# Choosing each token's two experts block by block instead of for all four blocks together

## The chip, the cores and the metric

The kernel runs on one core of a Trainium2 chip. The metric is device time in microseconds (us) of one execution. A core has five engines that run side by side, each through its own list of instructions in order: TensorE (PE in the profile, with PEld for its weight loads), VectorE (DVE), ScalarE (ACT), GpSimd (POOL) and SyncE (SP), which here issues the loads of the weights. An engine that waits for a semaphore holds up all that stands behind it in its list.

## The reference

One layer of an encoder over 512 tokens (and 16 meta tokens) of width 1024: a mixer of two attention branches, then a mixture of 32 experts in 4 groups of 8. The change is in the routing of the second half:

```python
g_logits = u @ w_group + b_group                 # 4 groups
p_grp, g_sel = top_k(softmax(g_logits), 1)       # one group per token
e_logits = (u @ w_router + b_router).reshape(n, 4, 8)
e_prob = softmax(e_logits[group g_sel])          # its 8 experts
p_exp, e_sel = top_k(e_prob, 2)                  # two experts per token
gate = p_grp * p_exp / sum(p_exp)
expert = g_sel * 8 + e_sel
out = sum over the two of gate * w2[expert] @ (silu(xe @ w1[expert]) * (xe @ w3[expert]))
```

Here u is the RMS norm of the stream h after the mixer. The experts hold 201 MB of float32 weights, and all of them are read.

## The kernel before

Tokens lie on the 128 partitions, in NB = 4 blocks of 128. The kernel is written as straight code on tiles; a planner puts most instructions of each engine in order by its own costs and by priority (program order, moved ahead by `high_priority(offset=...)`), one at a time as they become ready in its plan, and that order is then fixed. Only `stage_moe` keeps PE, ACT and DVE in the order in which it is written. Tiles come from pools with a number of buffers each: a tile that finds none free waits until one is released, and with it the engine that was to write it. What matters here are H (8 buffers of 2 KB a partition), A (4, two of them held by the gather targets X), the one PSUM buffer `av` and the two PSUM buffers `tr`, and the buffers R, W and P in which the weights land.

The steps around the change, in order of time:

- `stage_o` multiplies the mixer's output by w_o (L807), adds it to h (L820), half a block of 512 columns at a time, and gives each half to `router_half`, ahead of other work by an offset of 300.
- `router_half` (8 calls: 4 blocks, 2 halves each) multiplies the half by the norm's weights on POOL (L861, into an H tile u2) and writes it to DRAM, u2d, by a DMA that POOL issues (L862); squares it on ACT (L864, junk, an A tile); turns it on PE (L867) and copies it to SBUF on DVE (L869, hT, an A tile); multiplies by the router's weights into `av` (L872). After the first half DVE saves the partial logits (L874). After the second, DVE adds both squares (L877, L878), POOL takes the power -1/2 (L880), and DVE makes the logits lg of the block, 4 of groups and 32 of experts (L881, L882).
- `choose`, at an offset of 600, once the logits of all four blocks are there: on DVE the largest group logit (L891), the index of its group (L894 to L897), the other groups' experts pushed to -1e30 (L898, L900), the 8 largest values and their indices for each block (L905, L907), the two indices as floats ef (L909), their one-hot rows eh (L912, an H tile) and the sum of the two rows, os (L914). `columns` makes two more small tables (L931 to L935). PE then counts the tokens ahead of each one by 10 small matmuls into `av` (L919, L921), and DVE makes val, each token's place in its expert (L922).
- `stage_moe` makes from val the list of the first pair's tokens (L1043, L1048, L1050), starts the gather of their rows from u2d (L1054), runs 12 matmuls that keep PE at work (`busy`, L941), makes the tables of gates and indices (`gates`, `tables`: L947 to L999, the matmuls L986), 8 more matmuls of `busy`, turns the gathered rows (L1071, copied at L1077 and L1078), and then runs 16 pairs of experts (L1086 up, L1106 down, L1117 back to the tokens).
- The weights of the experts come in pieces of 512 KB (L140 on SP) in the order in which PE takes them. Each piece needs a free buffer of its kind, so loads run ahead until all buffers are full and go on when PE has used a piece.

Of the kernel before, what the change touches and what calls it, by code (L numbers as in the profile page):

```python
# [9 lines left out]
F32 = mybir.dt.float32  # L10
F32R = mybir.dt.float32r
F16 = mybir.dt.float16
BF16 = mybir.dt.bfloat16
I32 = mybir.dt.int32
U32 = mybir.dt.uint32
AF = mybir.ActivationFunctionType
ALU = mybir.AluOpType
AX = mybir.AxisListType
# [5 lines left out]
NB = 4  # L24
# [5 lines left out]
NEG = -1e30  # L30
# [5 lines left out]
C_ID, C_I128, C_COS, C_SIN, C_TOK, C_THR, C_TOKB, C_ONCE = 0, 128, 256, 296, 336, 344, 352, 360  # L36
# [36 lines left out]
class Body:  # L73
# [753 lines left out]
    def route_setup(self):  # L827
        nc, a, cs = self.nc, self.a, self.cs
        self.g2 = self.P([128, D], F32, "gffn")
        nc.scalar.dma_start(self.g2, a["norm_ffn_g"].partition_broadcast(128))  # L830
        wr = self.H([128, 8, 36], F32, "wr0")
        nc.scalar.dma_start(wr[:, :, 0:4], a["w_group"].rearrange("(c p) n -> p c n", p=128))
        nc.scalar.dma_start(wr[:, :, 4:36], a["w_router"].rearrange("(c p) n -> p c n", p=128))
        gt = self.S([128, 8], F32, "g2t")
        with nc.allow_non_contiguous_dma(reason="small"):
            nc.scalar.dma_start(gt, a["norm_ffn_g"].rearrange("(c p) -> p c", p=128))
        self.wr = self.H([128, 8, 36], F32, "wr")
        nc.vector.tensor_tensor(self.wr, wr, gt.unsqueeze(2).to_broadcast([128, 8, 36]), ALU.mult)
        self.rt = self.cp.tile([128, 1344], F32, name="route", tag="score", bufs=1)
        self.trib = self.rt[:, 672:736].bitcast(BF16)  # L840
        nc.vector.tensor_scalar(self.trib, cs[:, C_I128:C_I128 + 128], cs[:, C_TOK:C_TOK + 1], None, op0=ALU.is_ge)
        self.onesb = self.C([128, 128], BF16, "onesb")
        nc.gpsimd.memset(self.onesb, 1.0)
        self.lg = self.rt[:, 0:144].rearrange("p (b n) -> p b n", b=NB)
        self.lgs = self.rt[:, 144:288].rearrange("p (b n) -> p b n", b=NB)
        self.val = self.rt[:, 288:416].rearrange("p (b e) -> p b e", b=NB)
        self.lm = self.rt[:, 416:544].rearrange("p (b e) -> p b e", b=NB)
        self.io512 = self.rt[:, 772:1284]
        for b in range(NB):
            nc.gpsimd.tensor_scalar(self.io512[:, 128 * b:128 * b + 128], cs[:, C_I128:C_I128 + 128],  # L850
                                    128.0 * b + 1.0, None, op0=ALU.add)
        self.br = self.rt[:, 736:772]
        nc.scalar.dma_start(self.br[:, 0:4], a["b_group"].partition_broadcast(128))
        nc.scalar.dma_start(self.br[:, 4:36], a["b_router"].partition_broadcast(128))

    def router_half(self, b, nh, h):

        nc = self.nc
        cols = slice(512 * nh, 512 * nh + 512)
        u2 = self.H([128, 512], F32, "u2")  # L860
        nc.gpsimd.tensor_tensor(u2, h, self.g2[:, cols], ALU.mult)  # L861
        nc.gpsimd.dma_start(self.u2d[128 * b:128 * b + 128, cols], u2)  # L862
        junk = self.A([128, 512], F32, "junk")
        nc.scalar.activation(junk, h, AF.Square, accum_out=self.ss[:, b, nh:nh + 1])  # L864
        p = self.tr()
        for i in range(4):
            nc.tensor.transpose(p[:, 128 * i:128 * i + 128], h[:, 128 * i:128 * i + 128], self.idt)  # L867
        ut = self.A([128, 4, 128], F32, "hT")
        nc.vector.tensor_copy(ut.rearrange("p c n -> p (c n)"), p)  # L869
        lp = self.av()[:, 0:36]  # L870
        for c in range(4):
            nc.tensor.matmul(lp, ut[:, c, :], self.wr[:, 4 * nh + c, :], start=(c == 0), stop=(c == 3))  # L872
        if nh == 0:
            nc.vector.tensor_copy(self.lgs[:, b, :], lp)  # L874
            return
        ms = self.S([128, 1], F32, "ms2")
        nc.vector.tensor_tensor(ms, self.ss[:, b, 0:1], self.ss[:, b, 1:2], ALU.add)  # L877
        nc.vector.tensor_scalar(ms, ms, 1.0 / D, EPS, op0=ALU.mult, op1=ALU.add)  # L878
        rs = self.rs[:, b:b + 1]
        nc.gpsimd.tensor_tensor(rs, ms, self.nhalf, ALU.pow)  # L880
        nc.vector.tensor_tensor(self.lgs[:, b, :], lp, self.lgs[:, b, :], ALU.add)  # L881
        nc.vector.scalar_tensor_tensor(self.lg[:, b, :], self.lgs[:, b, :], rs, self.br, op0=ALU.mult, op1=ALU.add)  # L882

    def choose(self):

        nc, cs = self.nc, self.cs
        io = cs[:, C_I128:C_I128 + 128]
        lg4, lg32 = self.lg[:, :, 0:4], self.lg[:, :, 4:36]
        n4 = [128, NB, 4]
        gm = self.gm = self.S([128, NB], F32, "gm", bufs=1)  # L890
        nc.vector.reduce_max(gm, lg4, axis=AX.X)  # L891
        t4 = self.S(n4, F32, "t4")
        i4 = io[:, 0:4].unsqueeze(1).to_broadcast(n4)
        nc.vector.tensor_tensor(t4, lg4, gm.unsqueeze(2).to_broadcast(n4), ALU.is_lt)  # L894
        nc.vector.scalar_tensor_tensor(t4, t4, 8.0, i4, op0=ALU.mult, op1=ALU.add)
        gi = self.S([128, NB], F32, "gi")
        nc.vector.tensor_reduce(gi, t4, axis=AX.X, op=ALU.min)  # L897
        nc.vector.tensor_tensor(t4, i4, gi.unsqueeze(2).to_broadcast(n4), ALU.not_equal)  # L898
        n48 = [128, NB, 4, 8]
        nc.vector.scalar_tensor_tensor(self.lm.rearrange("p b (g e) -> p b g e", g=4), t4.unsqueeze(3).to_broadcast(n48), NEG,  # L900
                                       lg32.rearrange("p b (g e) -> p b g e", g=4), op0=ALU.mult, op1=ALU.add)
        self.e8 = self.S([128, NB, 8], F32, "e8", bufs=1)
        ix = self.S([128, NB, 8], U32, "ix")
        for b in range(NB):
            nc.vector.max(self.e8[:, b, :], self.lm[:, b, :])  # L905
        for b in range(NB):
            nc.vector.max_index(ix[:, b, :], self.e8[:, b, :], self.lm[:, b, :])  # L907
        ef = self.ef = self.S([128, NB, 2], F32, "ef", bufs=1)
        nc.vector.tensor_copy(ef, ix[:, :, 0:2])  # L909
        n8 = [128, NB, 2, 32]  # L910
        eh = self.eh = self.H(n8, F32, "eh")
        nc.vector.tensor_tensor(eh, io[:, 0:32].unsqueeze(1).unsqueeze(1).to_broadcast(n8), ef.unsqueeze(3).to_broadcast(n8), ALU.is_equal)  # L912
        self.os = self.C([128, NB, 32], BF16, "os")
        nc.vector.tensor_tensor(self.os, eh[:, :, 0, :], eh[:, :, 1, :], ALU.add)  # L914
        self.columns()
        pp = self.av()
        for b in range(NB):
            o = pp[:, 32 * b:32 * b + 32]
            nc.tensor.matmul(o, self.trib, self.os[:, b, :], start=True, stop=(b == 0))  # L919
            for bb in range(b):  # L920
                nc.tensor.matmul(o, self.onesb, self.os[:, bb, :], start=False, stop=(bb == b - 1))  # L921
        nc.vector.scalar_tensor_tensor(self.val, pp[:, 0:128].rearrange("p (b e) -> p b e", b=NB), 1.0, self.os,  # L922
                                       op0=ALU.add, op1=ALU.mult)
# [486 lines left out]
```

## Time and profile before

| | |
|---|---|
| median of 3 runs | 1018.7 us (1017.58 to 1022.35) |
| the profiled execution, its own time | 1022.12 us |
| its span in the trace | 1020.3 us |
| PE busy | 943.5 us, 92% of the span |
| DVE busy | 533.3 us, 52% |
| ACT busy | 340.8 us, 33% |
| POOL busy | 193.1 us, 19% |
| DMA | 253.60 MB, 249 GB/s on average |
| largest parts of the chain that ended last | PE L1086 17%, DMA of in_w 13% |

Times within the trace are counted from the start of the span. The profiled execution is 3.4 us above the median, and 1.8 us of its time lie outside the span. Lines (L807) are those of the kernel before.

### The profile page before, as it was taken

To read this page: it belongs to the slowest core of one execution; us is meant where nothing else is said; L and a number is where in the kernel's file an instruction comes from. 1 tells how busy PE (TensorE), PEld (TensorE's weight loads), DVE (VectorE), ACT (ScalarE), POOL (GpSimd) and SP (SyncE) were. 2 spreads that over 40 slices of the span, in tenths; PEclk is the share of its full clock that TensorE was granted. 3 is DMA by queue.
4 is the path that set the end of the run, shared out by engine and by line. 5 is a ranking of instruction groups with operands and counts; after the bars stand their busy time and mean duration, and the time that the engine had idled before them with its cause. 6 is when DMAs were issued, how large, how long until landed. Compare 5 with 4: busy or idle time off the path is not lost.

```text
span 1020.3 us, 13274 instructions
## 1 busy us (share of the span) xinstructions
PE 943.5 (92%) x4794; PEld 589.6 (58%) x4795; DVE 533.3 (52%) x1050; ACT 340.8 (33%) x671; POOL 193.1 (19%) x223
## 2 busy tenths in 40 slices
PE   6889898999998999889979999999999999999994
PEld 5878897778897887768833434444433333333331
DVE  7559999998727578763541252333322223222232
ACT  6156645566545575551211111111111111111014
POOL 4320050705241100150620111111100111000003
PEclk7799899999998999999979999999999999999998
DMA  9100021414252133179939999999999999999982
GB/s 302 38 22 22 22 63 42 124 32 134 68 155 73 63 124 125 63 243 388 364 120 409 409 408 408 408 409 408 408 409 408 408 408 406 409 407 409 409 334 84
DMA packets 108403, 253.60 MB, mean 249 GB/s; under 512 B 16664, under 2 KB 48672, under 8 KB 108336
## 3 DMA queue, kind: packets, MB, share of 16 engines
q1 hardware_dynamic: 94208, 233.70, 60.3%
q10 hardware_dynamic: 11040, 12.22, 3.6%
q0 software_dynamic: 3088, 6.82, 1.8%
q8 instruction: 38, 0.62, 0.2%
q14 instruction: 29, 0.24, 0.1%
HBM read 248.51 MB, written 8.39 MB: 252 GB/s over the span
## 4 chain that ended last, share of the span: by engine, by line
PE 58%; DMA 16%; DVE 16%; ACT 4%; issue 3%; POOL 2%; ACTq 0%; POOLq 0%; SPq 0%; DVEq 0%
PE mm L1086 17%; DMA raw<-in_w 13%; PE mm L1106 6%; PE mm L1117 5%; PE mm L778 4%; PE mm L380 4%; PE mm L807 3%; PE mm L391 3%; DVE E L679 3%; DVE score L547 2%; PE av L592 2%; PE tr L1099 2%; PE mm L499 2%; DVE m L546 2%; DMA raw<-in_w_in 2%
## 5 line engine op out<-in xcount | busy, mean ns | idle before, releaser
L1086 PE MATMUL mm<-raw,xs 128*64 128x512 f32 x1024 | 246.2, 601 | 10.5 <-DMA raw<-in_w 10.2
L1086 PEld LDWEIGHTS mm<-raw,xs 128*64 128x64 f32 x1024 | 66.2, 136 | 140.6 <-issue 114.6
L391 PE MATMUL mm<-uH,w 128*128 128x512 f32 (+1 forms) x448 | 128.8, 368 | 2.5 <-DVE w L168 2.5
L177 DVE SCALAR_TENSOR_TENSOR Y<-mm,tab,Y 128x512 fp32r<-128x512 f32 x32 | 24.0, 750 | 187.4 <-ACT Y L176 185.8
L1106 PE MATMUL mm<-raw,hT 128*64 128x512 f32 x480 | 119.0, 595 | 2.5 <-DMA raw<-in_w 2.5
L1185 DVE TENSOR_TENSOR h<-mm,h 128x512 f32<-128x512 f32 x120 | 76.9, 681 | 55.5 <-PE mm L1117 55.5
L391 PEld LDWEIGHTS mm<-uH,w 128*128 128x128 f32 x448 | 81.1, 190 | 16.3 <-DVE w L168 2.9
L380 PE MATMUL mm<-w,uH 128*128 128x256 f32 (+1 forms) x448 | 86.8, 295 | 0.6 <-ACT uH L173 0.4
L1106 PEld LDWEIGHTS mm<-raw,hT 128*64 128x64 f32 x480 | 37.0, 137 | 79.4 <-issue 60.2
L391 PE MATMUL mm<-uL,w 128*128 128x512 f32 (+1 forms) x224 | 82.3, 367 | 0.0
L176 ACT ACTIVATE Y<-mm,tab 128x512 fp32r<-128x512 f32 x32 | 22.0, 687 | 164.4 <-PE mm L1106 155.0
L380 PEld LDWEIGHTS mm<-w,uH 128*128 128x128 f32 x448 | 74.3, 203 | 1.7 <-ACT uH L173 0.8
L1117 PE MATMUL mm<-Y,ST 128*128 128x512 f32 x246 | 73.0, 419 | 0.0
L380 PE MATMUL mm<-w,uL 128*128 128x256 f32 (+1 forms) x224 | 66.0, 295 | 2.6 <-DVE uL L174 2.6
L1054 POOL DMA_INDIRECT X<-u2d,idx x15 | 15.8, 1053 | 267.3 <-PE tr L1071 266.8
L1090 ACT ACTIVATE g<-mm,rss 64x512 f32<-64x512 f32 x32 | 21.9, 685 | 121.3 <-PE mm L1086 121.3
L167 ACT ACTIVATE w<-raw 128x1024 fp32r<-128x1024 f32 (+1 forms) x54 | 55.3, 1048 | 14.6 <-DMA raw<-in_w_in 13.3
L1117 PEld LDWEIGHTS mm<-Y,ST 128*128 128x128 f32 x246 | 41.6, 188 | 31.6 <-issue 13.8
L168 POOL TENSOR_TENSOR w<-raw,w 128x1024 fp32r<-128x1024 f32 x20 | 48.8, 2452 | 42.0 <-ACT w L167 21.6
L1092 DVE SCALAR_TENSOR_TENSOR hid<-mm,rss,g 64x512 f32<-64x512 f32 x32 | 23.8, 743 | 59.6 <-ACT g L1090 59.6
L168 DVE TENSOR_TENSOR w<-raw,w 128x1024 fp32r<-128x1024 f32 (+1 forms) x34 | 44.9, 1337 | 7.1 <-ACT w L167 4.4
L380 PEld LDWEIGHTS mm<-w,uL 128*128 128x128 f32 x224 | 45.2, 202 | 3.0 <-DVE uL L174 3.0
(329 smaller groups left out, 1523.7 us busy)
## 6 DMA issues: line engine op xcount, KB each, us to landing
raw<-in_w SPq DMA_DIRECT2D x384, 512.0 KB, 10.2
raw<-in_w_in SPq DMA_DIRECT2D x36, 512.0 KB, 4.4
gate<-gst ACTq DMA_DIRECT2D x16, 256.0 KB, 2.5
gate<-gate ACTq DMA_DIRECT2D x8, 512.0 KB, 5.8
raw<-in_w_o SPq DMA_DIRECT2D x8, 512.0 KB, 5.7
x<-in_x SPq DMA_DIRECT2D x4, 512.0 KB, 5.8
raw<-in_w_up_a SPq DMA_DIRECT2D x4, 512.0 KB, 5.0
raw<-in_w_up_b SPq DMA_DIRECT2D x4, 512.0 KB, 8.5
```

The costliest lines, as they stand in the source:

```text
L167: nc.scalar.activation(h, r, AF.Copy)
L168: (eng or nc.vector).tensor_tensor(l, r, h.bitcast(F32), ALU.subtract)
L177: self.nc.vector.scalar_tensor_tensor(lo, src, scale, hi.bitcast(F32), op0=ALU.mult, op1=ALU.subtract)
L380: nc.tensor.matmul(o, s, m[:, c % 4, :n], start=(c == 0 and k == 0), stop=(c == 7 and k == 2))
L391: nc.tensor.matmul(p[:, :x1 - x0], s[:, c, :], m, start=(c == 0 and k == 0), stop=(c == 7 and k == 2))
L679: nc.vector.tensor_tensor_scan(e, e, e, 0.0, ALU.add, ALU.max)
L778: nc.tensor.matmul(p, s, y[c][:, m, :], start=(c == 0 and k == 0), stop=(c == 3 and k == 2))
L807: nc.tensor.matmul(acc[b][nh], s, m[:, 0, 512 * nh:512 * nh + 512], start=(c == 0 and k == 0), stop=(c == 7 and k == 2))
L1086: self.nc.tensor.matmul(p[r:r + 64], xs[:, k, par], w[:, c, :], start=(k == 0), stop=(k == 7))
L1106: self.nc.tensor.matmul(o[n][64 * r:64 * r + 64], ht[:, r, c, :], w[:, 0, 512 * n:512 * n + 512], start=(c == 0), stop=(c == 3))
L1117: self.nc.tensor.matmul(ps, st[:, 128 * b:128 * b + 128], y[:, j, :], start=(first and j == 0), stop=(j == 1))
L1185: self.nc.vector.tensor_tensor(h, ps[n], h, ALU.add)
```

## The change

The body of `choose` up to os is taken out of it and made for one block at a time, in `choose_block(b)`, which `router_half` calls behind the logits of its block, so inside the priority of that function (offset 300). It leaves `columns`, the matmuls and val in `choose`. The tiles that outlive a block (gm, e8, ef, eh, os) are made in `choose_setup`, called from `route_setup`, together with i8, a constant row of 0, 1/8, 2/8, 3/8. With i8 the search for the group's index takes one instruction less: a comparison and the index are added in one step, and the push to -1e30 is made on 4 columns before it is spread over the 32.

```diff
@@ route_setup
+        self.choose_setup()
@@ router_half
         nc.vector.scalar_tensor_tensor(self.lg[:, b, :], self.lgs[:, b, :], rs, self.br, op0=ALU.mult, op1=ALU.add)
+        self.choose_block(b)
+
+    def choose_setup(self):
+        nc, io = self.nc, self.cs[:, C_I128:C_I128 + 128]
+        self.gm = self.S([128, NB], F32, "gm", bufs=1)
+        self.e8 = self.S([128, NB, 8], F32, "e8", bufs=1)
+        self.ef = self.S([128, NB, 2], F32, "ef", bufs=1)
+        self.eh = self.H([128, NB, 2, 32], F32, "eh")
+        self.os = self.C([128, NB, 32], BF16, "os")
+        self.i8 = self.S([128, 4], F32, "i8", bufs=1)
+        nc.vector.tensor_scalar(self.i8, io[:, 0:4], 0.125, None, op0=ALU.mult)
+
+    def choose_block(self, b):
+
+        nc, i8 = self.nc, self.i8
+        lg4, lg32 = self.lg[:, b, 0:4], self.lg[:, b, 4:36]
+        gm = self.gm[:, b:b + 1]
+        nc.vector.reduce_max(gm, lg4, axis=AX.X)
+        t4 = self.S([128, 4], F32, "t4")
+        nc.vector.scalar_tensor_tensor(t4, lg4, gm, i8, op0=ALU.is_lt, op1=ALU.add)
+        gi = self.S([128, 1], F32, "gi")
+        nc.vector.tensor_reduce(gi, t4, axis=AX.X, op=ALU.min)
+        no = self.S([128, 4], F32, "no")
+        nc.vector.tensor_scalar(no, i8, gi[:, 0:1], NEG, op0=ALU.not_equal, op1=ALU.mult)
+        lm = self.lm[:, b, :]
+        nc.vector.tensor_tensor(lm.rearrange("p (g e) -> p g e", g=4), no.unsqueeze(2).to_broadcast([128, 4, 8]),
+                                lg32.rearrange("p (g e) -> p g e", g=4), ALU.add)
+        ix = self.S([128, 8], U32, "ix")
+        nc.vector.max(self.e8[:, b, :], lm)
+        nc.vector.max_index(ix, self.e8[:, b, :], lm)
+        ef, eh = self.ef[:, b, :], self.eh[:, b]
+        nc.vector.tensor_copy(ef, ix[:, 0:2])
+        n = [128, 2, 32]
+        nc.vector.tensor_tensor(eh, self.cs[:, C_I128:C_I128 + 32].unsqueeze(1).to_broadcast(n), ef.unsqueeze(2).to_broadcast(n), ALU.is_equal)
+        nc.vector.tensor_tensor(self.os[:, b, :], eh[:, 0, :], eh[:, 1, :], ALU.add)
 
     def choose(self):
 
-        nc, cs = self.nc, self.cs
...
-        nc.vector.tensor_tensor(self.os, eh[:, :, 0, :], eh[:, :, 1, :], ALU.add)
+        nc = self.nc
         self.columns()
         pp = self.av()
```

## Rows read from the trace of the kernel before

**Rows 1.** The page: the span in 40 equal slices, bytes moved.

```profile
GB/s 302 38 22 22 22 63 42 124 32 134 68 155 73 63 124 125 63 243 388 364 120 409 409 408 408 408 409 408 408 409 408 408 408 406 409 407 409 409 334 84
```

**Rows 2.** Stretches: us, PE, PEld, DVE, ACT, POOL busy (x), PE clock, DMA share, GB/s.

```profile
499.90:510.40 10.50, 8.26 (x60) 7.66 (x60) 6.08 (x22) 3.17 (x10) 4.32 (x7) 0.84 0.98 348
...
506.00:508.00 2.00, 1.41 (x9) 1.27 (x9) 1.42 (x7) 0.32 (x2) 0.76 (x3) 0.77 1.06 426
508.00:510.00 2.00, 1.76 (x8) 1.64 (x9) 0.20 (x1) 0.00 (x0) 0.49 (x1) 0.50 0.99 387
...
514.00:516.00 2.00, 0.71 (x18) 0.57 (x19) 1.38 (x5) 0.00 (x0) 0.00 (x0) 0.50 0.00 0
...
526.00:528.00 2.00, 2.00 (x12) 0.72 (x10) 0.00 (x0) 0.00 (x0) 1.54 (x3) 1.00 0.03 8
```

**Rows 3.** The chain that ended last, 484 to 530 us: start, us, what.

```profile
506.30 1.26 PE av L872 x8
...
507.85 1.92 PE av L872 x8
...
516.06 4.85 PE mm L941 x11
...
524.35 0.46 PE tr L1071 x4
```

**Rows 4.** Timeline, DVE and PE, the choice: start, us, instruction, [idle before].

```profile
510.39 0.17 DVE L891 TENSOR_REDUCE gm<-route 128x4 f32<-128x16 f32 x1
511.42 0.29 DVE L900 SCALAR_TENSOR_TENSOR route<-t,route 128x128 f32<-128x128 f32 x1
511.75 0.47 DVE L905 MAX8 e<-route 128x8 f32<-128x32 f32 x4
512.62 0.07 DVE L907 MATCH_VALUE_LOAD ix<-e,route 128x8 f32 x1
512.89 0.17 DVE L909 CAST ef<-ix 128x8 f32<-128x8 uint32 x1
513.10 0.42 DVE L912 TENSOR_TENSOR eh<-const,ef 128x256 f32<-128x256 f32 x1
513.44 0.17 DVE L931 TENSOR_SCALAR par<-ef 128x8 f32<-128x8 f32 x1
513.56 0.29 DVE L914 TENSOR_TENSOR os<-eh 128x128 bf16<-128x128 f32 x1
513.90 0.21 PE L919 MATMUL av<-os,route 128*128 128x32 bf16 x2 [4.15 <-DVE os L914]
514.37 0.29 DVE L922 SCALAR_TENSOR_TENSOR route<-av,os 128x128 f32<-128x128 f32 x1
```

**Rows 5.** Timeline, small DVE instructions, and DVE's and POOL's work before them.

```profile
504.82 1.27 POOL L861 TENSOR_TENSOR u<-h,gffn 128x512 f32<-128x512 f32 x1
505.26 0.88 DVE L882 SCALAR_TENSOR_TENSOR route<-route,rs 128x36 f32<-128x36 f32 x1
509.79 0.20 DVE L881 TENSOR_TENSOR route<-av,route 128x36 f32<-128x36 f32 x1 [1.95 <-PE av L872]
510.09 0.26 DVE L882 SCALAR_TENSOR_TENSOR route<-route,rs 128x36 f32<-128x36 f32 x1
515.93 0.17 DVE L947 TENSOR_TENSOR gd<-route,gm 128x16 f32<-128x16 f32 x1
516.01 0.16 DVE L948 TENSOR_TENSOR gd<-e 128x8 f32<-128x8 f32 x1
```

**Rows 6.** Timeline, POOL and SP: the last copy to u2d, the gather, the loads.

```profile
506.39 0.61 POOL L862 DMA_DIRECT2D u2d<-u  x1 [0.30 <-POOL u L861]
...
516.30 1.19 POOL L1054 DMA_INDIRECT X<-u2d,ixr  x1 [7.81 <-DVE gd L948]
527.50 4.30 SPq L140 DMA_DIRECT2D raw<-in_w  x6
```

**Rows 7.** The line L862 in 506 to 507 us: its DMA.

```profile
DMA to landing us min/median/max: 6.3/6.3/6.3
```

More of the change, by code (lines that the diff above doesn't have):

```diff
@@ L882, in router_half @@
         nc.vector.scalar_tensor_tensor(self.lg[:, b, :], self.lgs[:, b, :], rs, self.br, op0=ALU.mult, op1=ALU.add)
-    def choose(self):
-        nc, cs = self.nc, self.cs
[L887 to L913, printed above, removed]
-        nc.vector.tensor_tensor(self.os, eh[:, :, 0, :], eh[:, :, 1, :], ALU.add)
```

## The prediction

> **What bounds the kernel now.** Start with the bytes moved in 40 slices of the span [rows 1]. From the 22nd slice (535 us) on the DMA engines move 408 GB/s without a break until the last two slices, so the expert half ends when the weights have come, whatever the engines do meanwhile. In front of it stands a hole: the 21st slice has 120 GB/s. The stretches [rows 2] show where: nothing moves in 514 to 516 us, 8 GB/s in 526 to 528. All buffers are full; the first new load of that run is issued at 527.50 [rows 6], when PE has used the first pieces. The end is therefore the moment at which the experts start, plus a fixed number of bytes at a fixed rate. Each microsecond by which the experts start earlier or later moves the end by one, and this holds until the hole, some 15 us, is used up.
>
> The chain [rows 3] says what leads to that start: the router's matmuls (L872), the choice on DVE, the matmuls that count (L919), the first list, then from 516.06 a fixed run of PE work to the turning at 524.35. The timeline of the choice [rows 4] is a row of dependent DVE instructions from 510.39, behind the logits of the last block, to os, with PE starting at 513.90. These 3.51 us are the ones that the change is about. The clock has nothing to add here: PE is at half clock there already [rows 2], and has little to do, and 516.06 onward is moved as a whole.
>
> **What the change takes off the path.** Behind the last logits only block 3 is left to choose. I take each step from start to start. The steps from 510.39 to 511.42 are five of 16 columns, 1.03 us or 0.206 each; the change has four, of 4 columns: 0.82. The push (L900, 128 columns) takes 0.33; from 0.206 at 16 columns to 0.33 at 128 is 1.1 ns a column, so 32 columns take 0.22. Four maxima and four index searches take 511.75 to 512.89; one search is 512.62 to 512.89, 0.27, and one maximum, as a step of the small kind, 0.21. The float copy is 0.21 (512.89 to 513.10). eh, with 64 columns instead of 256, 0.26 by the same slope; os, with 32 instead of 128, about 0.24 until PE starts (0.34 now). Sum 0.82 + 0.22 + 0.21 + 0.27 + 0.21 + 0.26 + 0.24 = 2.23 us, against 3.51: 1.28 us less. Of PE's 10 matmuls, 0.47 us from 513.90 to the DVE step at 514.37, six need only blocks 0 to 2 and can run before; I take 0.15 us for them (0.02 to 0.05 each). Together **1.43 us** come off. The instruction for i8 (about 0.17 us of DVE) depends on constants alone and lies somewhere in DVE's idle time; POOL, ACT and SP get no instruction.
>
> **What it puts in front.** Blocks 0 to 2 now choose inside the router's part, with 11 DVE instructions each: 33 where the old form had 21 in all, behind everything. Alone, as a dependent row, a block takes those 2.2 us. DVE's busy time from 499.90 to 510.40 is 6.08 of 10.50 us [rows 2]: 4.42 us are idle, 1.95 of them in one piece before the last L881 [rows 5]. The three blocks want at most 3 x 2.2 = 6.6 us. But instructions that don't depend on each other start 0.08 us apart, though each lasts 0.16 (515.93 and 516.01) [rows 5], so in the shadow of a 0.69 us copy (L869) or of another block's chain an added one costs 0.08: 33 x 0.08 = 2.6 us. So 2.6 to 6.6 us have to go into 4.42.
>
> Who waits behind them? In DVE's list stand L869, L874, L877, L878 and L881 of the halves still to come; PE waits for them through `av`, `tr` and the A tiles, and no stage has spare time: L872 of half (3,0) starts at 506.30 behind an L881. The delay of the last logits is bounded by 0 (all in idle time) and 4.65 us (all three chains in one piece in front of these, less the 1.95 that the last gap takes). The order of the list decides. The row that shows how the planner orders such a chain is par (L931): written behind os, it stands between eh (513.10) and os (513.56), in the pause that the dependence leaves. So a copy that is ready gets in after one small instruction and not after eleven. With five halves still to come, each held up once by one small instruction of 0.08 to 0.2, the delay is 0.4 to 1.0 us; I take **0.6**. Both ends, 0 and 4.65, stay for the range.
>
> Here a page speaks against the change. The timeline shows L882 take 0.88 us at 505.26, while POOL's multiplication L861 runs from 504.82 to 506.09; the same instruction takes 0.26 at 510.09 with POOL idle [rows 5]. The Trainium skill ("SBUF — State Buffer", section "Who interferes with whom") says that a DVE instruction with two SBUF inputs contends with a GpSimd instruction that reads SBUF, and the loser waits for all of it; the rows agree. Four of each block's eleven have two SBUF inputs (t4, lm, eh, os). The old ones ran with POOL idle; now blocks 0 to 2 run beside the last L861. One L861 is left in that stretch and already costs 0.62 us there, so I add nothing; the price if it meets another chain instead is in a rival.
>
> A second page would make the sum smaller. "VectorE: DVE Perf Modes", "Rules for kernel authors", advises to keep the count of DVE operations low, since the pipeline is emptied after each. By it each of the 33 would cost its full 0.17 us, an estimate of 5.6 us, 1.2 over the idle time; the result would then be a gain of 0.2 us. The starts 0.08 apart are against it.
>
> **Sum.** 1.43 - 0.6 = 0.83 us earlier. The profiled execution would take 1022.12 - 0.8 = 1021.3; on the median, 3.4 us lower, 1018.7 - 0.8 = **1017.9 us**.
>
> **The rivals.**
>
> *The chains stand in front of the router (slower).* Blocks 0 to 2 are earlier in the program than the later halves and have the same offset, so they come first wherever both are ready. If three or more small instructions stand in front of each critical one, the delay passes 1.43 us, and this is the point from which the change loses. With 2.2 to 4.65 us the result is 0.8 to 3.2 us slower: 1019.5 to 1021.9. PE would also thin out: its clock is at 0.77 in 506 to 508 and 0.50 after, and the L872 run goes from 1.26 to 1.92 us with it [rows 2, 3]; one more run at half clock is 0.66. For it: 6.6 us against 4.42. Against: L931.
>
> *POOL's last multiplication moves.* eh holds one of the 8 H buffers from block 0 on, so the eighth u2 may get its buffer later and L861 meet the chains of blocks 1 and 2 between 506 and 510. A DVE instruction that loses waits up to 1.27 us [rows 5]: 1.43 - 0.6 - 1.27 is 0.4 us slower, 1019.1. The gather is not at risk: its copy is issued at 506.39 and lands after 6.3 us [rows 6, 7], 3.6 us before the gather.
>
> *The gain is hidden anyway.* The experts' start could depend on the gathered rows rather than on the choice. The copy lands at 512.7 and the rows are turned behind a run of PE work at 524.35, so only a shift of L862 by over 3 us would do it. 1018.7.
>
> *The plan comes out otherwise.* One more early DVE instruction and a longer-lived H tile can turn an order in another stage; either sign, 2 to 6 us.
>
> **How the numbers follow.** Forecast 0.42 (its own range, with a delay of 0 to 1.4 us, 1017.3 to 1018.7); chains in front 0.28; POOL 0.10; hidden 0.08; another plan 0.12, half for each sign. A third of a per cent covers all but the last, and the three runs differ by more (1017.58 to 1022.35), so about 1 us is added below and little above: 1015.5 to 1022.3, which leaves out most of the other plans and the end of the chains. A measurement of this kernel can tell about 0.5%, 5.1 us, from no change. Only another plan goes so far: faster 0.03, slower 0.05, within 0.92.
>
> **What would show it.** Right: in the changed trace os of block 3 is done about 2.2 us after its logits, six counting matmuls stand before it, L869 and L881 of later halves start within 0.2 us of their PE or ACT release, and the first load after the hole is issued some 0.8 us earlier. Wrong: DVE without idle time between 500 and 510 and PE waiting for L869 or L874; an L861 behind 506.4; a first busy matmul (L941) later than 516.06; or a stage before 484 us that has moved.

## The result and the profile after

| | before | after |
|---|---|---|
| median of 9 runs each, same chip | 1017.58 us (1012.31 to 1022.35) | 1024.14 us (1019.35 to 1025.17) |
| ratio of the means | | 1.0053 (1.0034 to 1.0071): about 5.4 us slower (3.5 to 7.2) |
| the profiled execution, its span | 1022.12, 1020.3 us | 1019.35, 1017.6 us |

The two profiled executions mislead: the slower kernel has the shorter span. Its router stage starts 6.45 us earlier (490.22 against 496.67 us). PE's granted clock in 26 to 51 us was 0.99 there and 0.80 before, long ahead of the change, and this goes the same way; but e3, the changed kernel run again, has 0.77 there and starts at 493.48, so what sets the start stays open. Over all profiles of this study that start lies between 488.5 and 498.1 us. So the stage is measured from its own first matmul. Line numbers of after: L861, L862, L869, L872, L880 to L882 are now L862, L863, L870, L873, L881 to L883, and the choice is L901 (gm), L903 (t4), L905 (gi), L907 (no), L909 (lm), L912 and L913 (the two largest), L915 (ef), L917 (eh), L918 (os), L930 (val). L941 is L949, L1086 is L1094.

| us, from the first L873 | last L882 | last logits (L883) | val | first expert matmul |
|---|---|---|---|---|
| before | 13.12 | 13.42 | 17.70 | 28.86 |
| after | 17.59 | 20.22 | 23.25 | 33.51 |
| after, second profile (e3) | 17.59 | 20.22 | 23.24 | 34.03 |
| eh in the route tile (e1) | 13.30 | 13.60 | 16.62 | 26.97 |

Each row is read from one execution. The experts start 4.65 to 5.17 us later in the stage, which is what the times show. The two values belong to one kernel: they part behind val, in the first run of `busy` (4.33 and 4.85 us), so the columns up to val compare two kernels more closely than the last one. What lies behind has not changed: the first load after the hole is issued 1.97 us behind the first expert matmul before and 1.96 after, and from it to the end of the span are 492.8 and 491.9 us.

The delay is in front of the choice. POOL's timeline after (start, us, instruction, what its idle time waited for):

```profile
482.00 1.29 POOL L862 TENSOR_TENSOR u<-h,gffn 128x512 f32<-128x512 f32 x1 [0.17 <-DVE h L820]
...
494.89 0.55 POOL L881 TENSOR_TENSOR rs<-ms,nhalf 128x1 f32<-128x1 f32 x1 [5.26 <-DVE gi L905]
495.41 4.95 POOL L862 TENSOR_TENSOR u<-h,gffn 128x512 f32<-128x512 f32 x4
500.76 0.55 POOL L881 TENSOR_TENSOR rs<-ms,nhalf 128x1 f32<-128x1 f32 x1 [0.40 <-DVE gi L905]
501.27 1.27 POOL L862 TENSOR_TENSOR u<-h,gffn 128x512 f32<-128x512 f32 x1
...
503.11 1.28 POOL L862 TENSOR_TENSOR u<-h,gffn 128x512 f32<-128x512 f32 x1
```

And POOL's before, of which the last one stands in [rows 5]:

```profile
490.51 1.30 POOL L861 TENSOR_TENSOR u<-h,gffn 128x512 f32<-128x512 f32 x1
...
497.82 1.27 POOL L861 TENSOR_TENSOR u<-h,gffn 128x512 f32<-128x512 f32 x1
```

Before, seven of the eight multiplications for u2 have started 1.2 us into the stage, and one is left. After, only two have: the other six start 5.2 to 12.9 us into it, four of them in one piece, in the middle of DVE's work for the router. DVE's timeline shows what that does:

```profile
495.69 1.04 DVE L909 TENSOR_TENSOR route<-no,route 128x32 f32<-128x32 f32 x1
...
496.94 1.02 DVE L883 SCALAR_TENSOR_TENSOR route<-route,rs 128x36 f32<-128x36 f32 x1
...
498.71 0.45 DVE L915 CAST ef<-ix 128x2 f32<-128x2 uint32 x1
...
499.14 1.24 DVE L903 SCALAR_TENSOR_TENSOR t<-route,gm,i 128x4 f32<-128x4 f32 x1
...
500.41 0.21 DVE L917 TENSOR_TENSOR eh<-const,ef 128x64 f32<-128x64 f32 x1
...
501.36 1.20 DVE L907 TENSOR_SCALAR no<-i,gi 128x4 f32<-128x4 f32 x1
...
502.61 1.83 DVE L909 TENSOR_TENSOR route<-no,route 128x32 f32<-128x32 f32 x1
...
507.81 0.20 DVE L882 TENSOR_TENSOR route<-av,route 128x36 f32<-128x36 f32 x1 [1.59 <-PE av L873]
507.92 0.25 DVE L883 SCALAR_TENSOR_TENSOR route<-route,rs 128x36 f32<-128x36 f32 x1
...
510.33 0.19 DVE L918 TENSOR_TENSOR os<-eh 128x32 bf16<-128x32 f32 x1
510.44 0.25 DVE L883 SCALAR_TENSOR_TENSOR route<-route,rs 128x36 f32<-128x36 f32 x1
...
513.47 0.29 DVE L930 SCALAR_TENSOR_TENSOR route<-av,os 128x128 f32<-128x128 f32 x1 [0.16 <-PE av L929]
```

Two things are to be seen. The first six take 0.17 to 0.25 us each where POOL is idle (L909 at 511.62 takes 0.19), and each of them ends with one of POOL's multiplications: 499.14 + 1.24 = 500.38, and 495.41 + 4.95 = 500.36. Together they are 5.5 us too long. (The last of the six starts 0.50 us ahead of its multiplication, while POOL issues a copy at 502.48; what holds it in that half microsecond is not shown.) And in the last block the two logits instructions stand apart: 507.92 is block 2's, with its whole choice behind it, and block 3's own comes at 510.44, 2.63 us behind its L882, where before it was 0.30. The power for block 2 (L881 at 500.76) stands in POOL's list behind the four multiplications, and in DVE's list block 2's logits, with the eleven instructions behind them, stand after the router's last L882. That the second follows from the first is read from the lists; it was not tried apart.

PE after, in the same stretch, and its windows (columns as in [rows 2]):

```profile
496.89 1.37 PE L873 MATMUL av<-wr,hT 128*128 128x36 f32 x8 [0.38 <-DVE route L882]
498.93 1.08 PE L868 MATMUL tr<-const,h 128*128 128x128 f32 x4 [0.67 <-DVE hT L870]
500.54 1.92 PE L873 MATMUL av<-wr,hT 128*128 128x36 f32 x8 [0.52 <-DVE route L875]
...
505.86 1.92 PE L873 MATMUL av<-wr,hT 128*128 128x36 f32 x8 [1.19 <-DVE ms L879]
...
514.77 4.33 PE L949 MATMUL mm<-route,idb 128*128 128x512 bf16 x12
```

```profile
496.00:498.00 2.00, 1.62 (x13) 1.38 (x11) 2.00 (x6) 0.72 (x2) 2.00 (x3) 0.88 1.03 414
498.00:500.00 2.00, 1.33 (x6) 0.83 (x5) 2.00 (x6) 0.72 (x2) 2.00 (x2) 0.50 0.81 322
```

DVE is busy all of the time (2.00 of 2.00 us in both windows), PE waits for it, and PE's granted clock falls to 0.50, its lower level of 1.2 GHz, 7 us into the stage. Before it fell 10 us into it [rows 2]. The last four router runs take 1.37, 1.92, 1.92 and 1.92 us instead of 1.06, 0.98, 1.25 and 1.92.

By these rows the 6.80 us of delay are 2.33 of block 2's choice in front of the last logits (2.63 less 0.30) and 4.47 up to the last L882. Of the 4.47 the router runs are longer by 1.92; the other 2.55 hold the waits, and also a turning at half clock (L868 at 498.93, 1.08 us against 0.63 at full clock). That is a sum and not yet a cause. In e3, the same kernel, the clock fell later, and the first of the four runs was as fast as before:

```profile
500.15 1.08 PE L873 MATMUL av<-wr,hT 128*128 128x36 f32 x8 [0.38 <-DVE route L882]
```

Yet its last L882 came at the same 17.59 us, so this one run's 0.29 us was not on the path. How far waits and clock can be told apart is what the experiments had to show.

### The profile page after: what moved, and what is told of

It is laid out like the page before. It is cut to its first block, busy times and chain, and to the rows that moved or that the text cites. A ratio compares the mean times of both kernels' runs of the same rounds, so it can differ in the third digit from the quotient of the medians.

```text
span 1017.6 us, 13290 instructions
## 1 busy us (share of the span) xinstructions
PE 941.5 (93%) x4795; PEld 587.5 (58%) x4795; DVE 538.9 (53%) x1074; ACT 340.4 (33%) x671; POOL 194.4 (19%) x223
## 4 chain that ended last, share of the span: by engine, by line
PE 61%; DMA 15%; DVE 15%; ACT 4%; issue 2%; POOL 1%; ACTq 0%; POOLq 0%; SPq 0%; DVEq 0%
PE mm L1094 17%; DMA raw<-in_w 13%; PE mm L1114 6%; PE mm L391 6%; PE mm L1125 5%; PE mm L778 4%; PE mm L380 3%; PE mm L807 3%; DVE E L679 2%; PE av L592 2%; PE mm L499 2%; PE tr L1107 2%; DVE score L547 2%; DVE m L546 1%; PE tr L1079 1%
## 5 line engine op out<-in xcount | busy, mean ns | idle before, releaser
L1094 PE MATMUL mm<-raw,xs 128*64 128x512 f32 x1024 | 246.0, 601 | 10.4 <-DMA raw<-in_w 10.0
L1094 PEld LDWEIGHTS mm<-raw,xs 128*64 128x64 f32 x1024 | 66.2, 136 | 140.7 <-issue 115.5
L380 PE MATMUL mm<-w,uH 128*128 128x256 f32 (+1 forms) x448 | 83.3, 287 | 1.5 <-DVE w L168 0.7
L380 PEld LDWEIGHTS mm<-w,uH 128*128 128x128 f32 x448 | 71.0, 194 | 2.7 <-DVE w L168 0.9
L380 PE MATMUL mm<-w,uL 128*128 128x256 f32 (+1 forms) x224 | 63.9, 286 | 1.0 <-DVE uL L174 1.0
L391 PEld LDWEIGHTS mm<-uL,w 128*128 128x128 f32 x224 | 42.4, 189 | 6.6
```

The costliest lines, as they stand in the source:

```text
L380: nc.tensor.matmul(o, s, m[:, c % 4, :n], start=(c == 0 and k == 0), stop=(c == 7 and k == 2))
L391: nc.tensor.matmul(p[:, :x1 - x0], s[:, c, :], m, start=(c == 0 and k == 0), stop=(c == 7 and k == 2))
L1094: self.nc.tensor.matmul(p[r:r + 64], xs[:, k, par], w[:, c, :], start=(k == 0), stop=(k == 7))
```

## The experiments

Each was timed beside the kernel before on the same chip; "stage" is from the first router matmul to the first expert's.

**What moves POOL's multiplications.** The theory after the result: the H buffers are handed out in the order in which the program first writes the tiles. eh is first written in `choose_block(0)`, between the u2 of block 0 and those of block 1, so in the plan all six later u2 wait for eh's turn, which comes after block 0's choice. At run time nothing waits for eh: four of the six start at 495.41, 5.00 us before eh is first written (L917 at 500.41). What the plan has fixed is their place in POOL's list, behind the power of block 1 (L881 at 494.89). The rival is that eh's one buffer out of eight is missing (which touches only the last u2), or that the chains delay the router by themselves.

e1 puts eh into the route tile and leaves the rest of the change:

```diff
-        self.eh = self.H([128, NB, 2, 32], F32, "eh")
+        self.eh = self.rt[:, 544:672].bitcast(BF16).rearrange("p (b k e) -> p b k e", b=NB, k=2)
```

> The changed kernel, but the one-hot rows eh lie in free columns of the routing tile (as bf16) and not in one of the 8 H buffers; in the list of POOL the multiplications L862 stand again where they stood before the change, and the choice stays block by block. The stage is measured from the first router matmul to the first matmul of the experts: 28.9 us before, 33.5 after. Theory BUFFER (eh's place in the H buffers holds back POOL's multiplications of blocks 1 to 3 until they meet the choice): stage 27.9 to 28.7, time 0.2 to 1 us under before, ratio 0.998 to 1.000. Theory CHAINS (the choice's instructions themselves hold up the router's in DVE's list): stage 32 to 34, 3 to 5 us slower than before.

Measured: 0.9987 (0.9972 to 1.0002), stage 26.97 us. POOL and the end of DVE's choice:

```profile
486.78 1.29 POOL L862 TENSOR_TENSOR u<-h,gffn 128x512 f32<-128x512 f32 x1
...
501.15 1.26 POOL L862 TENSOR_TENSOR u<-h,gffn 128x512 f32<-128x512 f32 x1
```

```profile
501.54 0.92 DVE L883 SCALAR_TENSOR_TENSOR route<-route,rs 128x36 f32<-128x36 f32 x1
...
506.24 0.20 DVE L882 TENSOR_TENSOR route<-av,route 128x36 f32<-128x36 f32 x1 [0.16 <-PE av L873]
506.54 0.25 DVE L883 SCALAR_TENSOR_TENSOR route<-route,rs 128x36 f32<-128x36 f32 x1
```

POOL's list is that of before again: one multiplication is left late in the stage, and one DVE instruction waits for it, as in [rows 5]. The last logits come 13.60 us into the stage against 13.42, with the same 33 instructions of the choice in DVE's list. The chains alone therefore cost 0.18 us net. Up to val e1 is 1.08 us ahead of before (16.62 against 17.70). The same kernel run again (e7):

> The kernel of the first experiment again (eh in the routing tile), for a narrower interval. Its stage was 27.0 us against 28.9 before. Theory BUFFER: ratio 0.997 to 0.999. If the start of the execution hides it: 0.999 to 1.001.

Measured: 0.9988 (0.9969 to 1.0006), stage 27.10 us, the last logits at 13.52 us and val at 16.54. So val comes 1.08 and 1.16 us earlier, where the forecast had 0.83; neither time by itself is clear of no change.

e2 keeps eh an H tile, but writes it once early, so that only the missing buffer is left:

```diff
+        nc.vector.memset(self.eh, 0.0)
```

> The changed kernel with one more instruction: DVE clears eh where it is made, so that eh has its H buffer before the first product u2 asks for one. eh still takes one of the 8 buffers. Theory BUFFER, form TURN (it is the order in which the buffers are given out that holds back POOL): POOL's first six multiplications are early again, the seventh and eighth late; stage 28.5 to 30.5, time 0 to 1.5 us over before. Form COUNT (one buffer fewer is enough to hold POOL back): stage 32 to 34, as after. Theory CHAINS: 32 to 34.

Measured: 0.9999 (0.9977 to 1.0022), stage 28.23 us. Two multiplications are late and hit two instructions:

```profile
501.17 2.50 POOL L862 TENSOR_TENSOR u<-h,gffn 128x512 f32<-128x512 f32 x2
```

```profile
501.29 1.17 DVE L908 TENSOR_SCALAR no<-i,gi 128x4 f32<-128x4 f32 x1
...
502.58 1.15 DVE L910 TENSOR_TENSOR route<-no,route 128x32 f32<-128x32 f32 x1
```

So the missing buffer takes the gain and no more: val comes at 17.83 us, 1.21 behind e1 and 0.13 behind before, and the stage is 1.26 us longer than in e1. It is the order of the first writes that makes the rest; e4 and e6 try that order by itself.

e4 calls `choose_block` for all four blocks at the end, in `choose`, at its offset of 600:

```diff
@@ router_half
-        self.choose_block(b)
@@ choose
+        for b in range(NB):
+            self.choose_block(b)
```

> The new instructions of the choice for each block, 44 instead of 21, but all called behind the last block's logits, where the old choice stood. Nothing stands in front of the router; POOL's list is as before. If the four chains fill each other's pauses: 44 starts of about 0.09 us, 4.0 us against 3.5, stage 29 to 30, 0 to 1 us slower. If each instruction costs its full 0.17 us: 7.5 us, 4 us slower.

Measured: 0.9999 (0.9981 to 1.0018), stage 27.26 us. The expectation missed (29 to 30 us, nothing in front of the router): blocks 0 to 2 are chosen between the router's instructions here too (os of block 1 at 504.93, the last logits at 506.00), since the offset of 600 puts them first as soon as they are ready. But eh's first write now follows those of all u2, and POOL has its old list: the first multiplication of block 1 at 485.96. That is a second repair with the same tile in the same pool. Both repairs together (e8):

> As the kernel before this one, but with the four calls written behind the last block's logits, at the higher priority of that place (offset 600), where the planner still takes each block as its logits come. Theory BUFFER: stage 26.5 to 27.5 us, ratio 0.997 to 0.999. If the higher priority puts the chains in front of the router's instructions (theory CHAINS): stage over 28.

Measured: 0.9984 (0.9965 to 1.0002), 1.6 us under before (from 3.6 under to 0.2 over), stage 27.18 us. This is the lowest ratio found; its interval just reaches no change and overlaps that of e1.

The changed kernel itself, run again beside these (e3):

> The changed kernel itself again, for a second trace beside these. All theories: stage 33 to 34, time 4 to 6 us over before. If the difference came from the start of the execution (another clock there) and not from this stage: stage the same, time within 1 us of before.

Measured: 1.0054 (1.0026 to 1.0082), stage 34.03 us, and the same waits: L909 1.04, L883 1.02, L915 0.45, L903 1.23, L907 1.20, L909 1.83 us.

**Whether the late multiplications cost by their reads.** e5 leaves POOL's six instructions late, but they only clear u2 instead of multiplying, so the experts work on zeros:

```diff
-        nc.gpsimd.tensor_tensor(u2, h, self.g2[:, cols], ALU.mult)
+        nc.gpsimd.memset(u2, 0.0)
```

> The changed kernel with POOL's multiplication into u2 (L862) left out and a clearing of the same tile by POOL in its place, so the experts work on zeros; POOL's list has the same instructions in nearly the same late places, but they read nothing from SBUF. From the first router matmul to the last logits it is 13.4 us before and 20.2 after, to the first expert matmul 28.9 and 33.5. Theory PORT (DVE instructions that read SBUF twice wait for a multiplication that reads SBUF): no DVE instruction of the choice over 0.3 us, last logits after 13 to 15 us, stage 27 to 28.5. Theory LATE (POOL being late delays the norms and the copies, whatever it does there): stage 32 to 34 still.

Measured: 1.0008 (0.9988 to 1.0027), stage 28.57 us.

```profile
500.46 2.86 POOL L862 MEMSET u<- 128x512 f32 x6
```

```profile
500.76 0.18 DVE L909 TENSOR_TENSOR route<-no,route 128x32 f32<-128x32 f32 x1
...
501.45 0.26 DVE L883 SCALAR_TENSOR_TENSOR route<-route,rs 128x36 f32<-128x36 f32 x1
...
502.51 0.83 DVE L915 CAST ef<-ix 128x2 f32<-128x2 uint32 x1
...
502.65 0.70 DVE L903 SCALAR_TENSOR_TENSOR t<-route,gm,i 128x4 f32<-128x4 f32 x1
```

L909 and L883, which have two inputs in SBUF, take 0.18 and 0.26 us beside the clearing, where they took 1.04 and 1.02 beside a multiplication. A CAST waits, until the clearing ends at 503.3, and the three instructions that start behind it, L903 among them, end with it. With nearly the same order of the lists, 4.9 to 5.5 us of the stage are gone. But the clearings are also shorter, 2.86 us for six against 4.95 for four multiplications, so the stage alone does not tell the reads from the length of POOL's work; the single instructions do, for L909 and L883. What is left over e1 is 1.60 us: 0.90 are the order (the last L882 is followed by its L883 after 1.20 us, 0.30 in e1, with the end of block 2's choice between them), 0.41 come up to that L882, where the CAST's wait lies, and 0.29 behind the logits. The Trainium skill ("SBUF — State Buffer", section "Who interferes with whom") says that a DVE instruction with two SBUF inputs contends with a GpSimd instruction that reads SBUF and not with one that only writes it, and that a cast or a tensor_scalar can contend too, when its operands meet the conditions of a mode that takes both ports. The traces agree: L883 is 1.02 us beside a multiplication and 0.26 beside the clearing, L915 waits beside both, and L907, a TENSOR_SCALAR, waited 1.20 us in after.

**Whether late multiplications alone are enough.** e6 is the kernel before with an H tile that is first written behind block 0's logits, as eh is, and read in `choose`:

```diff
+        self.hold = self.H([128, 256], F32, "hold")
@@ router_half, behind the logits
+        if b == 0:
+            nc.vector.tensor_copy(self.hold[:, 0:36], self.lg[:, 0, :])
@@ choose, behind os
+        nc.vector.tensor_copy(self.lgs[:, 0, :], self.hold[:, 0:36])
```

> The kernel before with its choice for all blocks, and one H tile that is first written (36 columns) behind the logits of block 0 and read at the end; in POOL's list the multiplications 3 to 7 then stand late, behind the first power, as they do after the change. Theory PORT: almost no DVE instruction with two SBUF inputs stands beside them, so the stage grows by 0 to 2 us over 28.9. Theory LATE: it grows by 4 to 5 us, to 33 or more.

Measured: 1.0042 (1.0022 to 1.0062), stage 32.11 us. So with the old choice, too, an H tile that is first written at that place is enough to make the kernel 4.3 us slower (2.2 to 6.3). Its multiplications start at 487.90, 5.04 us before `hold` is first written (L885 at 492.94): here too it is their place in POOL's list, and no wait for a buffer. How the planner comes to that list was not followed step by step; e1, e2, e4 and e6 change what is written first, and the list goes with it. The stage lies between the two expected cases, and only one instruction of DVE waited long.

```profile
487.90 4.96 POOL L862 TENSOR_TENSOR u<-h,gffn 128x512 f32<-128x512 f32 x4
```

```profile
491.55 1.36 DVE L883 SCALAR_TENSOR_TENSOR route<-route,rs 128x36 f32<-128x36 f32 x1
```

```profile
492.00:494.00 2.00, 0.71 (x7) 0.62 (x7) 1.97 (x8) 0.74 (x3) 0.90 (x2) 1.00 0.92 277
494.00:496.00 2.00, 2.00 (x12) 2.00 (x12) 0.64 (x2) 0.00 (x0) 2.00 (x3) 0.54 0.98 373
```

Behind that wait PE is busy for 0.71 us of 2, with one pause of 1.29 us, and right after it the granted clock is 0.54, then 0.50 for the rest of the router. The five later runs take 1.76, 1.76, 1.76, 1.93 and 1.92 us, where before they took 0.98, 1.06, 0.98, 1.25 and 1.92: 2.94 us more. With the wait's 1.10 that is 4.04, and the last L882 comes 3.99 us later.

**Clock or waits.** Two attempts. e9 (after), e10 (the kernel of e6) and e11 (that of e1) have 6 matmuls of `busy` behind each half from block 1 on:

```diff
+                if 2 * b + nh >= 2:
+                    with self.tc.high_priority(offset=300):
+                        self.busy(6)
```

> The changed kernel with six matmuls of busy put behind each half of the router's part from block 1 on (24 half-block runs become PE work that nobody needs; the router's and the experts' work is unchanged). POOL's multiplications stay where the changed kernel has them, so DVE should still wait for them as in its trace (L909 1.04, L883 1.02, L915 0.45, L903 1.24, L907 1.20, L909 1.83 us). CLOCK (a good part of the loss is that PE falls to half clock near 497.5, after which the router's runs take 1.92 us instead of 0.98 to 1.25): the clock stays nearer to 1 and the stage from the first router matmul to the first expert's goes from 33.5 to 34.0 us down to 31 to 32.5. WAITS (the waits alone make the loss): the stage stays at 33.5 or gets longer by what the added matmuls cost, 0.7 us for six at full clock.

> The kernel with the old choice and POOL's multiplications held back (stage 32.1 us, one DVE wait of 1.36 us, PE at half clock from 495 on), with six matmuls of busy behind each half from block 1 on. CLOCK: with the clock kept up the router's runs go from 1.76 to 1.93 us back to about 1.0 and the stage to 29.5 to 31 us. WAITS: the stage stays at 32 us or gets longer.

> The kernel with eh in the route tile (stage 27.0 to 27.1 us, no DVE wait for POOL) with the same added matmuls: the price of these where nothing is to be won but the half clock of the last halves. CLOCK: 26 to 27.5 us, since the last two or three router runs, at half clock there, go faster by 0.3 to 0.7 us each and the added work takes that back in part. WAITS: 27.5 to 29 us, the added work alone.

Measured: 1.0094 (1.0060 to 1.0128), 1.0066 (1.0035 to 1.0097), 1.0049 (1.0032 to 1.0065); stages 40.5, 34.2 and 32.3 us. Only e10 falls under one of its cases (WAITS, which had no upper bound). Six added matmuls had been priced at 0.7 us; eleven recorded ones take 2.76 us in e9. The matmuls depend on nothing, so the plan put them ahead of the waits rather than into them (in e9 34 of them are recorded, all from 489.9 to 502), and they cost 5.3 us by themselves (32.3 against 27.0). In e10 five multiplications ran off beside them and no DVE instruction waited, so e10 says nothing of the clock. e9 does tell the order of events:

```profile
502.00:504.00 2.00, 2.00 (x16) 1.78 (x15) 1.90 (x5) 0.24 (x1) 2.00 (x2) 1.00 0.43 115
504.00:506.00 2.00, 0.48 (x4) 0.29 (x2) 2.00 (x5) 0.49 (x2) 2.00 (x3) 0.92 0.91 287
506.00:508.00 2.00, 2.00 (x11) 2.00 (x11) 0.48 (x3) 0.33 (x1) 2.00 (x3) 0.50 0.90 277
```

POOL's six multiplications start at 501.75 with PE full and its clock at 1.00; then PE waits for DVE; then the clock falls.

e12 (after) and e13 (the kernel of e1) use matmuls that can't be planned ahead, because they read the half's own hT:

```diff
+        if 2 * b + nh >= 2:
+            p = self.mm()
+            for c in range(4):
+                nc.tensor.matmul(p[:, 0:128], ut[:, c, :], self.io512[:, 0:128], start=True, stop=True)
```

> The changed kernel with four more matmuls of 128 columns behind the router's run of each half from block 1 on, from the same turned half hT, so that they can't be moved ahead of it; nobody reads them. POOL's multiplications stay late and DVE should wait for them as before. CLOCK (the half clock makes a good part of the loss): PE is busier through the waits, its clock falls later than near 7 us into the stage, and the stage from the first router matmul to the first expert's is 31 to 33 us in place of 33.5 to 34.0. WAITS: the clock falls with the first long wait all the same, or stays up without gain, and the stage is 34 to 38 us, longer by the added runs (0.6 us each at full clock, 1.1 at half, for six).

> The kernel with eh in the route tile and the same added matmuls: their price where DVE doesn't wait for POOL. Stage 27 us without them. CLOCK: 27 to 28.5 us, since the last router run, at half clock there, takes 1.0 us again in place of 1.92. WAITS: 28.5 to 31 us. The difference between this stage and that of the padded changed kernel is the loss from the waits where the clock is treated alike; without padding it is 6.5 to 7.1 us.

Measured: 1.0090 (1.0056 to 1.0125) with a stage of 40.4 us, more than either theory had, and 1.0019 (0.9981 to 1.0056) with 29.0 us, as WAITS had it. The lists of PE are alike in the two, so their stages can be laid side by side. PE in e12 and in e13 (L877 are the added matmuls):

```profile
504.84 1.08 PE L873 MATMUL av<-wr,hT 128*128 128x36 f32 x8 [1.70 <-DVE route L886]
507.38 2.07 PE L877 MATMUL mm<-route,hT 128*128 128x128 f32 x8 [1.45 <-DVE hT L870]
...
516.92 1.76 PE L873 MATMUL av<-wr,hT 128*128 128x36 f32 x8
```

```profile
507.60 1.14 PE L877 MATMUL mm<-route,hT 128*128 128x128 f32 x8
...
512.58 0.98 PE L873 MATMUL av<-wr,hT 128*128 128x36 f32 x8
```

And the waits that opened PE's two pauses in e12, DVE:

```profile
500.92 1.29 DVE L919 CAST ef<-ix 128x2 f32<-128x2 uint32 x1
502.24 1.25 DVE L921 TENSOR_TENSOR eh<-const,ef 128x64 f32<-128x64 f32 x1
503.53 1.15 DVE L922 TENSOR_TENSOR os<-eh 128x32 bf16<-128x32 f32 x1
...
504.89 1.64 DVE L887 SCALAR_TENSOR_TENSOR route<-route,rs 128x36 f32<-128x36 f32 x1
```

Up to 507.38 and 507.60, with the clock at 1.00 in both until 506, e12 has lost 12.79 - 9.53 = 3.3 us to the waits. From there to the last router run PE has no pause in e12 (2.00 of 2.00 in each window from 508 to 516), no DVE instruction waits for POOL by more than 0.1 us, and the clock is 0.50 against 1.00: 9.54 us against 4.98, so 4.6 us are the clock. Behind it another 3.6 are lost (18.06 against 14.48), of which 1.6 are block 2's choice in front of the last logits (1.88 us from L886 to L887 against 0.30), 0.8 the last router run and 1.1 the first run of `busy`, 5.28 us against 4.14 (its length differs by 0.5 between the two profiles of the changed kernel). In this padded pair, then, the waits come first and cost the smaller part; the larger is the clock that follows them. In the changed kernel without padding PE is not busy throughout at half clock, so its own 4.47 us can't be cut as cleanly: the rows give 1.92 and 2.55, and how much of the waits hides beside the longer runs stays open.

e13 has one DVE wait of the same size, and there the clock stays:

```profile
503.18 1.30 DVE L913 TENSOR_TENSOR route<-no,route 128x32 f32<-128x32 f32 x1
```

```profile
504.00:506.00 2.00, 1.86 (x17) 1.75 (x16) 1.86 (x8) 0.72 (x2) 0.43 (x1) 1.00 0.92 285
```

PE had added matmuls to run meanwhile. In these traces, then, the clock falls behind the pause on PE and not behind the wait on DVE as such.

## Why the prediction was wrong

The forecast was 0.8 us faster and within 0.5%; the result is slower by 0.53%, a case that had a chance of 0.05 and was put down to another plan alone.

*The step that failed* is the delay of the last logits, taken as 0.6 us with bounds of 0 and 4.65. It is 6.80. The bound was made from added instructions, each at its duration of before; but these durations hold only beside the work that they ran beside. Two sentences carry the error. "One L861 is left in that stretch … so I add nothing" took POOL's list of before for that of after, where six are in that stretch. And the rival "POOL's last multiplication moves" named the mechanism (eh is an H tile, L861 meets the chains) but counted buffers: one of eight is gone, so only the eighth u2 moves, at one collision of up to 1.27 us. e2 tries this rival: against e1 it costs 1.26 us of stage, with two late multiplications and not one, and its time (0.9999, 0.9977 to 1.0022) has the priced 0.4 us of loss within its interval. What the rival left out is that a tile takes its turn in the order of first writes, and that eh's turn lies behind block 0's choice, in front of six u2. The prediction also counted four of a block's eleven instructions as able to meet POOL; in after a CAST (L915) and a TENSOR_SCALAR (L907) waited too.

*The rival "chains in front of the router"* had the sign and a part of the cause. Block 2's choice does stand in front of the last logits, for 2.33 us, and PE loses its clock earlier; but not because blocks 0 to 2 come first wherever they are ready. With POOL's list restored the chains cost 0.18 us (e1) and 0.10 (e7), less than the 0.6 of the forecast, and blocks 1 and 2 are chosen in each other's pauses. What the row of par (L931) [rows 4] was read to say holds. The Trainium skill ("VectorE: DVE Perf Modes", section "Rules for kernel authors") advises to keep the count of DVE operations low, and by it the prediction estimated 5.6 us for the 33 instructions; in e1 they cost 0.18 us, so this case does not show that price.

*The clock.* "The clock has nothing to add here" holds for the tail and was wrong for the router: in e6 2.9 of its 4.0 us are longer runs at half clock. The prediction priced one more run at half clock, 0.66 us, within the rival; the longer runs make 1.92 us in after, 1.64 in e3 and 2.94 in e6, not all of it on the path.

*Right:* the tail, 4.28 to 3.03 us from the last logits to val, 1.25 against 1.43 (1.09 on DVE, from 3.81 to 2.72, against 1.28; 0.16 on PE against 0.15). The steps of 4 columns take 0.19 to 0.26 us, not 0.206. That the experts' start sets the end: 492.8 and 491.9 us from the first new load to the end. That the gather is not at risk. From val to the first expert 11.16 us became 10.26 in after and 10.35 in e1, but 10.79 in e3, the kernel of after. The first run of `busy` takes 4.85 us before [rows 3], 4.33 in after and 4.85 in e3, so most of that gain goes with the execution and not with the change.

The signs named as "wrong" were there: DVE without idle time, PE waiting for the copies, multiplications of u2 late in the router, a stage before 484 us that had moved. The first matmul of `busy` comes 24.55 us into the stage against 19.39, though at 514.77 in the trace's own time.

## What to carry to other kernels

Where tiles of one pool are handed out in program order, a tile first written in the middle of a loop can move back, in the planner's order, all that the later passes take from that pool, not just one of them; so for each tile that a change moves, look which queue takes its buffers from the same pool and what then moves in that queue. A duration read from a trace belongs to the neighbours it had: before using it, ask what the other engines will run beside it after the change. And where PE's clock falls behind a short pause in a row of small matmuls, a wait of a microsecond is not priced at a microsecond.

## What the runs showed of the hardware

- One DVE wait of 1.36 us in a row of router matmuls and the pause of 1.29 us that it made on PE were followed by a granted clock of 0.50 for the rest of the router, and the last L882 came 3.99 us later than before (e6). With the router padded so that PE had hardly a pause, the clock stayed at 1.00 through all eight runs, beside a DVE wait of 1.30 us too (e13).
- A CAST with a single input of 128x2 waited for POOL's multiplication (1.29 us in e12) and even for a clearing, which has no input (0.83 us in e5), where two-input instructions did not wait for the clearing (0.18 and 0.26 us).
